# GLA norm ahead of the attention's splits, the window's pool lying first, and bonus rows loaded early, in a two-block fp32 kernel

## The chip, the cores and the metric

The kernel runs on one core of one Trainium2 chip. The metric is device time in microseconds; the time before is 2362.28 us, the median of three runs.

## The reference, cut to what matters

Two blocks run on a sequence of 1024 rows of width 1024, all in fp32. The first block (differential and stick-breaking attention, cross attention, MLP) is not touched by the change. The second block projects a normed input and mixes three things, whose outputs stand side by side in front of the last product:

```python
attn = _sliding_window_attention(aq, ak, av, sinks) * silu(ag)   # window of 128, bias by distance, a sink per head
rwkv = _rwkv7_mixer(h, rr, rk, rv, ...) * silu(rg)               # y + bonus, recurrence over time
gla = _gla_mixer(h, gq, gkk, gv, ...) * silu(gg)                 # gated linear attention, 4 heads
y = jnp.concatenate([attn, rwkv, gla], axis=-1) @ w_out
return x + gate[:, None] * _rmsnorm(y, g_post)
```

Linear attention (GLA) ends with a norm of its own: `o = o * rsqrt(mean(o*o, -1) + 1e-5) * norm_w`, with the mean over the 64 values of a head.

## The kernel before, in words

**Arithmetic.** Large products are made of three matmuls (`mm3`, L208 to L210) on operands split into a high part (ACT copies it, L200 for weights) and the rest (a subtraction, L201, on POOL in the second block). A weight piece comes by a DMA into `stg`, is split into `wh` (8 buffers, hence four pieces), and feeds twelve matmuls. PSUM has 8 banks.

**Order of work.** The second block runs its 1024 rows in two halves (c = 0, 1). The work is written as generators that issue instructions and yield costs; `weave(main, fill, ratio)` lets a filling stream of products (projections, output products) run beside a main stream that is a chain of small steps. The order of the main parts is: `g_rec(0)` (RWKV, then GLA, of the first half), the first attention window, `g_rec(1)`, and the second window with the output product (`g_tail`). At build time a scheduler orders each engine's instructions from this; on the chip each engine's queue runs in that order. All loads and stores are issued by SP, in one queue in order.

**A half of the recurrences.** `g_rec` opens the pool `rp` (with RWKV's tile `XT`), and when the first part is through, `gp` for GLA behind it. RWKV's `out(pr)` (L1910 on) loads two bonus rows (from `bd` and `pd`, tiles "t2"), multiplies them into the two output rows `yf` (L1917, L1918) and stores these to `yd`. GLA makes its score tile AT level by level, seven levels: `dist` (L2096 to L2098), `rows` (L2104), `gram` (L2115: 16 small matmuls a level, into one bank for each head, shared by two levels), `put` (L2127: a masked copy of each head's bank into AT). Then come a transpose (L2164, copied by L2166), the state (L2173 to L2179) and the output (L2186, L2189, copied out by L2193) into slots 4 and 5 of an eight-slot tile, `s.go`, whose slots 0 to 3 held AT.

**The norm.** `g_gla_out` (L2200 on) squares the output (L2209, ACT, into es), sums it by matmuls (L2214), takes the power (POOL, L218), broadcasts (L2217, ACT, into rb), multiplies by gate rows (sg, loaded by SP; L2220), makes rows of the broadcast by 8 matmuls on the identity (L2225), multiplies (L2226) and stores to `yd`. Its es, sg and rb are three tiles of tag "wp" from the window's pool `mx`.

**A window.** `win_load` loads one K row and four Q rows (`ws` tiles, also tag "wp"; in the second window also the last 128 columns of the half before) and splits them: `stack_k` (L455, L456 on ACT, L457 on DVE) and four `stack_q` (L441 twice on ACT, L442 twice on DVE). `g_window` issues the 1 MB bias table into slots 0 to 3 of `s.go`, runs the norm, and then eight units (`w_units`: 4 blocks of 128 rows by 2 groups of heads). A unit has scores (L1664, L1665), bias and maximum (L1667, L1668), exponentials (L1675), a normalisation of "wp" (L1681 on ACT for two heads, L1682 on POOL for two), transposes (L1696, copied by L1699), the product with V (L1706) and the gate (L1708).

**Where the window's pool lies.** In the first window `pp` (filling work: RWKV's preparation for the other half) is opened outside of `mx`, so `mx` lies behind it, over GLA's tiles. `g_window0` draws all of `win_load` in one go ahead of everything and yields -2000:

```python
with s.tc.tile_pool(name="mx", bufs=1, reuse_waits="tile") as mx:
    for _ in s.win_load(mx, 0):
        pass
    yield -2000
    yield from s.g_window(0)
```

In the second window `g_tail` allocates the tile `yw` first, runs `win_load` with its yields, then `g_window(1)`.

Of the kernel before, what the change touches and what calls it, by code (L numbers as in the profile page):

```python
# [12 lines left out]
F32 = mybir.dt.float32  # L13
F32R = mybir.dt.float32r
# [8 lines left out]
P = 128  # L23
D = 1024
T = 1024
KT = D // P
CH = 512
# [109 lines left out]
def chain(*gens):  # L137
    for g in gens:
        yield from g
# [29 lines left out]
class K:  # L169
# [1118 lines left out]
    def block2(s, wp, pre, out):  # L1288
        tc, nc = s.tc, s.nc
        with tc.tile_pool(name="b2", bufs=1, reuse_waits="tile") as b2, tc.tile_pool(name="wk3", bufs=2, reuse_waits="tile") as s.wk, tc.tile_pool(  # L1290
            name="smC", bufs=4, reuse_waits="tile"
        ) as s.sm:
            s.vt = b2.tile([P, NB, 400], F32, name="vt")
            s.b2_consts(b2)
            with tc.tile_pool(name="lo", bufs=1, reuse_waits="tile") as s.lop:
                with tc.tile_pool(name="wt", bufs=1, reuse_waits="tile") as wt:
                    with tc.tile_pool(name="pp", bufs=2, reuse_waits="tile") as pp:
                        vt = s.vt_load(wt, wp)

                        def beside(m):  # L1300
                            if m == 1:
                                hi = s.tl(s.xp, [P, KT, CH], "act", F32R)
                                lo = s.lop.tile([P, KT, CH], F32R, tag="lo1", name="lo1")
                                s.slow = s.fin_steps(1, hi, lo, s.wk)
                            for _ in range(2 if m >= 2 else 0):
                                next(vt, None)
                            if m == 7:
                                for _ in vt:
                                    pass

                        for _ in chain(s.g_p2a(pp, 0, pre, beside), s.g_vt()):
                            pass
                rest = s.g_p2b(1)
                weave(
                    s.g_rec(0), chain(s.g_p2b(0), s.take(rest, s.K0)),
                    0.25
                )
                with tc.tile_pool(name="pp", bufs=2, reuse_waits="tile") as pp:
                    weave(
                        s.g_window0(), chain(s.g_p2a(pp, 1), s.take(rest, s.K1)),  # L1320
                        0.9
                    )
                    while s.steps:
                        s.steps.pop(0)()
                tp = ExitStack()

                def tail():
                    yield from s.g_tail(tp.enter_context(tc.tile_pool(name="tp", bufs=1, reuse_waits="tile")))

                main = chain(s.g_rec(1), tail())  # L1330
                rest = chain(rest, s.g_wout2(b2), s.g_wout2a(s.g_final0(b2, out)))
                weave(main, rest, 0.28, False)
                with tp, tc.tile_pool(name="fp", bufs=1, reuse_waits="tile") as fp:
                    s.finish(fp, wp, out, rest)
# [253 lines left out]
    def win_load(s, mx, c):  # L1588

        nc = s.nc  # L1590
        sink = mx.tile([P, 8], F32, name="sink")
        s.nc.sync.dma_start(sink, s.A["sink"])
        kst = [mx.tile([P, P + CH], F32R, name=s.nm("k2")) for _ in range(4)]
        q8 = s.tl(s.xp, [P, KT, CH], "act", F32R)
        st = [mx.tile([P, 2, CH], F32, tag="wp", name=s.nm("ws"), bufs=3) for _ in range(3)]
        t = [st[i // 2][:, i % 2, :] for i in range(6)]
        if c == 1:
            s.nc.sync.dma_start(t[5][:, :P], s.pd[s.AK * P : (s.AK + 1) * P, c * CH - P : c * CH])
        s.get_rows(t[4], s.pd, s.AK, c)
        for h in range(4):  # L1600
            s.get_rows(t[h], s.pd, s.AQ + h, c)
        yield 0
        if c == 1:
            s.stack_k(mx, t[5][:, :P], [k[:, :P] for k in kst])
        s.stack_k(mx, t[4], [k[:, P:] for k in kst])
        yield 0
        qst = []
        for h in range(4):
            qst.append(s.stack_q(mx, t[h], [q8[:, 2 * h, :], q8[:, 2 * h + 1, :]]))
            yield 0  # L1610
        s.win = mx, sink, kst, qst

    def g_window(s, c):

        one = s.go
        bias = one[:, 0:4, :].rearrange("p a (h w) -> p (a h) w", w=2 * P)
        s.nc.sync.dma_start(bias, s.A["c_bias"])
        mx, sink, kst, qst = s.win
        yield from s.g_gla_out(mx, c)
        if c == 1:  # L1620
            t = s.lop.tile([P, KT, CH], F32R, tag="lo1", name=s.nm("ya"))
            s.ya = s.y_rows([4, 5, 6, 7], 1, [t, t])
        tail = []
        first = [(2500, 2150)[c], (3130, 2500)[c]] + [0] * 6
        yield from s.g_units(s.w_units(mx, c, qst, kst, bias, sink, one), tail, first)
        yield from s.g_drain(tail)

    def g_window0(s):
        with s.tc.tile_pool(name="mx", bufs=1, reuse_waits="tile") as mx:
            for _ in s.win_load(mx, 0):  # L1630
                pass
            yield -2000
            yield from s.g_window(0)

    def g_tail(s, tp):

        s.yw = tp.tile([P, KT, CH], F32R, name="yw")
        for x in s.win_load(tp, 1):
            yield x
        yield from s.g_window(1)  # L1640

    def w_units(s, wn, c, qst, kst, bias, sink, one):

# [82 lines left out]
    def g_rec(s, c):  # L1726

        tile = dict(bufs=1, reuse_waits="tile")
        with s.tc.tile_pool(name="rp", **tile) as rp:
            with s.tc.tile_pool(name="ra", **tile) as ra:  # L1730
                early, late = s.rwkv(rp, ra, c)
                yield from early
            with s.tc.tile_pool(name="gp", **tile) as gp:
                gla = s._gla(gp, c)
                for x in late:
                    yield x
                    for _ in range(2):
                        yield next(gla, 0)
                yield from gla

    def rwkv(s, rp, ra, c):
# [17 lines left out]
        st = {"S": rp.tile([P, 2, HD], F32, tag="S", name=s.nm("S"), bufs=2)}  # L1759
# [139 lines left out]
        def s5(jj):  # L1899
# [9 lines left out]
                )  # L1909
            del s2[jj]  # L1910

        def out(pr):
            y = st["yf"][pr]
            bo, sg = s.tl(s.wk, [P, CH], "t2"), s.tl(s.wk, [P, CH], "t2")
            s.get_rows(bo, s.bd, pr, c)
            s.get_rows(sg, s.pd, s.RG + pr, c)
            V.scalar_tensor_tensor(y, bo, 0.5, y, ALU.mult, ALU.add)  # L1917
            V.tensor_tensor(y, y, sg, ALU.mult)  # L1918
            s.put_rows(s.yd, 4 + pr, c, y)
# [99 lines left out]
                out(pr)  # L2019
                yield 0  # L2020

        return early(), late()


    def g_gate(s, c):
# [171 lines left out]
        yield -1500  # L2197
        s.go = one

    def g_gla_out(s, pool, c):  # L2200

        nc = s.nc
        V, G = nc.vector, nc.gpsimd
        mm, act = nc.tensor.matmul, nc.scalar.activation
        es, sg, rb = [pool.tile([P, 2, CH], F32, tag="wp", name=s.nm("go"), bufs=3) for _ in range(3)]
        es, sg, o = [[t[:, i, :] for i in range(2)] for t in (es, sg, s.go[:, 4:6, :])]
        rb = rb.rearrange("p a (b y t) -> p (a b) y t", y=2, t=P)
        for z in range(2):
            act(es[z], o[z], AF.Square)  # L2209
        yield -2500  # L2210
        ps = s.ps([P, 4, 2, 2])
        for z, e in enumerate(es):
            for i in range(4):
                mm(ps[:, i, z, :], e[:, i * P : (i + 1) * P], s.b64[:, 0:65:64], start=True, stop=True)  # L2214
        r = s.sm.tile([P, 16], F32, tag="gr", name=s.nm("gr"))
        s.rsq(r, ps.rearrange("p a b c -> p (a b c)"), 1.0 / HD, 1e-5)
        act(rb.rearrange("p i z (h t) -> p (i z h) t", t=HD), r[:, :, None].to_broadcast([P, 16, HD]), AF.Copy)  # L2217
        for z in range(2):
            s.get_rows(sg[z], s.pd, s.GG + z, c)
            V.scalar_tensor_tensor(o[z], o[z], s.hv[:, 8:9], sg[z], ALU.mult, ALU.mult)  # L2220
        yield -8000
        for z in range(2):
            ps = s.ps()
            for i in range(4):
                mm(ps[:, i * P : (i + 1) * P], rb[:, i, z, :], s.ident, start=True, stop=True)  # L2225
            V.tensor_tensor(o[z], o[z], ps, ALU.mult)  # L2226
            s.put_rows(s.yd, 6 + z, c, o[z])
            yield 872
# [184 lines left out]
```

## Time and profile before

| | us |
|---|---|
| runs of the kernel before (three) | 2349.17, 2362.28, 2364.81 |
| median | 2362.28 |
| the profiled execution | 2355.43 |
| its span, first to last instruction | 2353.7 |

The profiled execution's span is 1.7 us below its time; all starts below are microseconds from the start of the span. PE is TensorE's matmuls, ACT ScalarE, DVE VectorE, POOL GpSimd, SP the engine that issues the transfers. In a timeline row "x6" means six instructions in a row, the second number is the time from the first's start to the last's end, and a bracket tells the idle time of the engine just ahead and what ended it. The granted clock is that of TensorE, 1.00 being full.

### The profile page before, as it was taken

What the parts mean: (1) busy time and instruction counts of PE and PEld (TensorE: products, weight loads), DVE (VectorE), ACT (ScalarE), POOL (GpSimd) and SP (SyncE); (2) the same over time, 40 slices, a digit from 0 to 9 for tenths busy, and PEclk for the clock granted to TensorE, in tenths of its full rate; (3) what the DMA queues carried; (4) which work ended last, traced back from release to release, by engine and by line L of the source; (5) the groups of instructions that cost most, each with busy time, mean ns of one, the idle gap of its engine ahead of it and who ended that gap; (6) DMA issues with size and microseconds to landing.
All of it is one profiled execution on the core that took longest, in us unless ns stands there. A gap on an engine that the chain in (4) does not pass through costs nothing. (4 is left out here: it accounts for less than half of the span.)

```text
span 2353.7 us, 34778 instructions
## 1 busy us (share of the span) xinstructions
PE 2243.8 (95%) x13056; PEld 1897.6 (81%) x13056; DVE 1288.1 (55%) x2312; ACT 1034.8 (44%) x2196; POOL 688.9 (29%) x1035
## 2 busy tenths in 40 slices
PE   8999999999999999999999999999999988999876
PEld 6898999988898888888888888887787776777655
DVE  6665656676754555422423422346845648656485
ACT  6655656674643424411311312344533337434463
POOL 4101100000400003565655650036322333224343
PEclk9999999999999999999999999999999889989898
DMA  4010010123241311222222221143333233443461
GB/s 135 23 46 23 28 41 28 46 77 123 65 140 54 99 36 50 75 76 74 80 76 79 76 68 51 49 134 121 120 121 103 92 99 108 145 143 102 145 214 37
DMA packets 116393, 200.06 MB, mean 85 GB/s; under 512 B 14048, under 2 KB 33792, under 8 KB 115456
## 3 DMA queue, kind: packets, MB, share of 16 engines
q1 hardware_dynamic: 111456, 184.72, 24.0%
q0 software_dynamic: 4768, 13.11, 1.8%
q8 instruction: 102, 1.67, 0.3%
q14 instruction: 67, 0.55, 0.1%
HBM read 163.70 MB, written 34.08 MB: 84 GB/s over the span
## 5 line engine op out<-in xcount | busy, mean ns | idle before, releaser
L208 PE MATMUL ps<-act,wh 128*128 128x512 f32 x1664 | 668.3, 404 | 9.4 <-ACT wh L200 5.5
L210 PE MATMUL ps<-act,wh 128*128 128x512 f32 x1664 | 659.4, 396 | 0.0
L209 PE MATMUL ps<-act,wh 128*128 128x512 f32 x1480 | 584.0, 395 | 3.2 <-DVE act L204 2.1
L200 ACT ACTIVATE wh<-stg 128x512 fp32r<-128x512 f32 x374 | 234.4, 629 | 593.5 <-PE ps L209 472.6
L208 PEld LDWEIGHTS ps<-act,wh 128*128 128x128 f32 x1664 | 318.6, 192 | 80.5 <-ACT wh L200 5.5
L210 PEld LDWEIGHTS ps<-act,wh 128*128 128x128 f32 x1664 | 318.3, 191 | 68.9 <-issue 0.5
L209 PEld LDWEIGHTS ps<-act,wh 128*128 128x128 f32 x1480 | 282.2, 191 | 60.9 <-DVE act L204 3.0
L201 DVE TENSOR_TENSOR wh<-stg,wh 128x512 fp32r<-128x512 f32 x260 | 197.0, 760 | 154.9 <-ACT wh L200 152.1
L201 POOL TENSOR_TENSOR wh<-stg,wh 128x512 fp32r<-128x512 f32 x114 | 158.3, 1393 | 348.8 <-ACT wh L200 315.5
L907 DVE TENSOR_TENSOR act<-ps,act 128x512 f32<-128x512 f32 x112 | 77.0, 689 | 176.7 <-PE ps L210 176.5
L546 DVE TENSOR_TENSOR_SCAN pw<-pw,zero 128x128 f32<-128x128 f32 (+7 forms) x64 | 86.8, 1357 | 82.9 <-POOL pw L542 78.1
L944 POOL TENSOR_TENSOR ad<-ad,cb 128x256 f32<-128x256 f32 x96 | 72.8, 759 | 143.0 <-DMA ad<-adaT 139.9
L247 POOL TENSOR_TENSOR nacc<-nacc,t 128x512 f32<-128x512 f32 x28 | 38.5, 1378 | 259.9 <-ACT t L246 255.5
L1144 DVE SCALAR_TENSOR_TENSOR t<-ps,Rm 128x512 f32<-128x512 f32 x64 | 44.0, 691 | 128.3 <-PE ps L210 127.6
L949 POOL TENSOR_TENSOR ad<-ad 128x128 f32<-128x128 f32 (+5 forms) x288 | 98.9, 343 | 16.8
L208 PE MATMUL ps<-hid,wh 128*128 128x512 f32 x256 | 101.2, 395 | 0.0
L210 PE MATMUL ps<-hid,wh 128*128 128x512 f32 x256 | 101.2, 395 | 0.0
L209 PE MATMUL ps<-hid,wh 128*128 128x512 f32 x256 | 101.0, 395 | 0.0
L1145 ACT ACTIVATE t<-t 128x512 f32<-128x512 f32 x64 | 40.4, 631 | 135.8 <-DVE t L1144 135.8
L208 PE MATMUL ps<-wh,act 128*128 128x256 f32 x320 | 96.1, 300 | 0.0
L210 PE MATMUL ps<-wh,act 128*128 128x256 f32 x320 | 91.5, 286 | 0.0
L209 PE MATMUL ps<-wh,act 128*128 128x256 f32 x320 | 91.2, 285 | 0.0
(512 smaller groups left out, 4658.5 us busy)
## 6 DMA issues: line engine op xcount, KB each, us to landing
stg<-w2f SPq DMA_DIRECT2D x84, 256.0 KB, 3.0
stg<-w_dn SPq DMA_DIRECT2D x80, 256.0 KB, 2.8
stg<-w_up SPq DMA_DIRECT2D x64, 256.0 KB, 2.8
ad<-adaT POOLq DMA_DIRECT2D x96, 128.0 KB, 2.6
stg<-w2o SPq DMA_DIRECT2D x32, 256.0 KB, 2.8
pd<-t SPq DMA_DIRECT2D x30, 256.0 KB, 2.3
t<-yd SPq DMA_DIRECT2D x26, 256.0 KB, 3.4
rkd<-RK SPq DMA_DIRECT2D x4, 1280.0 KB, 5.2
```

Of the source, the lines that this page charges most:

```text
L200: nc.scalar.activation(hi, src, AF.Copy)
L201: (eng or nc.vector).tensor_tensor(lo, src, hi.bitcast(F32), ALU.subtract)
L208: mm(out, lh, rh, start=first, stop=False)
L209: mm(out, lh, rl, start=False, stop=False)
L210: mm(out, ll, rh, start=False, stop=last)
L247: nc.gpsimd.tensor_tensor(acc, acc, t[:, :n], ALU.add)
L546: V.tensor_tensor_scan(m[:, :w][:, ::-1], m[:, :w][:, ::-1], s.zero.to_broadcast([P, w]), 1.0, ALU.mult, ALU.add)
L907: s.nc.vector.tensor_tensor(hh, ps, hh, ALU.add)
L944: tt(t, t, cb[:, 256 * y : 256 * y + 256], ALU.mult)
L949: tt(acc[:, n, z, :] if w == 2 else a, a, b, ALU.add)
L1144: V.scalar_tensor_tensor(t, ps, 0.0, R[:, c * CH : (c + 1) * CH], ALU.max, ALU.mult)
L1145: nc.scalar.activation(t, t, AF.Square)
```

## The change

Three things are changed. `mx` is opened ahead of `pp`, and `win_load` allocates its load tiles ahead of everything else in it. `g_window` now drives `win_load` and `g_gla_out` by turns: loads; squares; K splits; norm sums, power, broadcast and gate; Q splits; then the rest of the norm and, behind it, the bias table's load. `g_gla_out` takes its es, rb and sg from slots 0 and 1, 2 and 3, 6 and 7 of `s.go`. The bonus rows of RWKV's first output row are loaded into tiles of their own ("ro") as soon as `gp` is open; those of the second row are loaded in `out(1)` as before.

```diff
-                with tc.tile_pool(name="pp", bufs=2, reuse_waits="tile") as pp:
+                with tc.tile_pool(name="mx", bufs=1, reuse_waits="tile") as mx, tc.tile_pool(
+                    name="pp", bufs=2, reuse_waits="tile"
+                ) as pp:
                     weave(
-                        s.g_window0(), chain(s.g_p2a(pp, 1), s.take(rest, s.K1)),
+                        s.g_window(0, mx), chain(s.g_p2a(pp, 1), s.take(rest, s.K1)),
...
     def win_load(s, mx, c):
...
+        st = [mx.tile([P, 2, CH], F32, tag="wp", name=s.nm("ws"), bufs=3) for _ in range(3)]
+        t = [st[i // 2][:, i % 2, :] for i in range(6)]
         sink = mx.tile([P, 8], F32, name="sink")
...
-    def g_window(s, c):
+    def g_window(s, c, mx, yw=None):
 
         one = s.go
+        load, out = s.win_load(mx, c), s.g_gla_out(c)
+        yield next(load)
+        if yw:
+            s.yw = mx.tile([P, KT, CH], F32R, name="yw")
+        yield next(out)
+        yield next(load)
+        yield next(out)
+        for x in load:
+            yield x
+        yield from out
         bias = one[:, 0:4, :].rearrange("p a (h w) -> p (a h) w", w=2 * P)
         s.nc.sync.dma_start(bias, s.A["c_bias"])
         mx, sink, kst, qst = s.win
-        yield from s.g_gla_out(mx, c)
...
-    def g_window0(s):
...
     def g_tail(s, tp):
 
-        s.yw = tp.tile([P, KT, CH], F32R, name="yw")
-        for x in s.win_load(tp, 1):
-            yield x
-        yield from s.g_window(1)
+        yield from s.g_window(1, tp, True)
...
+        def rows(pr, t):
+            bo, sg = st["rows", pr] = t
+            s.get_rows(bo, s.bd, pr, c)
+            s.get_rows(sg, s.pd, s.RG + pr, c)
+
         def out(pr):
             y = st["yf"][pr]
-            bo, sg = s.tl(s.wk, [P, CH], "t2"), s.tl(s.wk, [P, CH], "t2")
-            s.get_rows(bo, s.bd, pr, c)
-            s.get_rows(sg, s.pd, s.RG + pr, c)
+            if pr == 1:
+                rows(1, [s.tl(s.wk, [P, CH], "t2") for _ in range(2)])
+            bo, sg = st["rows", pr]
...
-        es, sg, rb = [pool.tile([P, 2, CH], F32, tag="wp", name=s.nm("go"), bufs=3) for _ in range(3)]
+        es, rb, sg = [s.go[:, z : z + 2, :] for z in (0, 2, 6)]
```

The new lines shift the numbers: in the rows of the changed kernel the units' lines are 1 or 2 higher (L1696 is L1697), those of GLA 7 higher (L2127 is L2134, L2209 is L2216).

The first place is VectorE's queue at the end of the first GLA. Before, with the masked puts of levels 4 to 6 (their shapes end in 4x16, 2x32 and 64):

```order
L2127 COPY_PREDICATED act_16187<-gm_17200,ps_17666 128x4x4x16
L2127 COPY_PREDICATED act_16187<-gm_17200,ps_17667 128x4x4x16
L2127 COPY_PREDICATED act_16187<-gm_17200,ps_17664 128x4x2x32
L2127 COPY_PREDICATED act_16187<-gm_17200,ps_17665 128x4x2x32
L2127 COPY_PREDICATED act_16187<-gm_17200,ps_17666 128x4x2x32
L2127 COPY_PREDICATED act_16187<-gm_17200,ps_17667 128x4x2x32
L2127 COPY_PREDICATED act_16187<-gm_17200,ps_17717 128x4x64
```

And the same place of the changed kernel, where k and act on the left are the low parts of the window's K and Q rows:

```order
L2134 COPY_PREDICATED act_16187<-gm_17204,ps_17666 128x4x4x16
L457 TENSOR_TENSOR k_3185_17822<-ws_17817,k_3183_17820 64x512
L2134 COPY_PREDICATED act_16187<-gm_17204,ps_17667 128x4x4x16
L457 TENSOR_TENSOR k_3186_17823<-ws_17817,k_3184_17821 64x512
L442 TENSOR_TENSOR act_17824<-ws_17815,act_17824 64x512 x4
L442 TENSOR_TENSOR act_17824<-ws_17816,act_17824 64x512 x4
L2134 COPY_PREDICATED act_16187<-gm_17204,ps_17664 128x4x2x32
L2134 COPY_PREDICATED act_16187<-gm_17204,ps_17665 128x4x2x32
```

Ten subtractions of the window's splits, which stood behind the whole of GLA, now stand ahead of the puts of its last two levels.

The second place is ScalarE's queue around the squares of the first window's norm. Before:

```order
L2193 ACTIVATE act_16187<-ps_17792 128x512
L455 ACTIVATE k_3180_17817<-ws_17824 64x512
L456 ACTIVATE k_3180_17817<-ws_17824 64x512
L455 ACTIVATE k_3181_17818<-ws_17824 64x512
L456 ACTIVATE k_3181_17818<-ws_17824 64x512
L200 ACTIVATE wh_17933<-stg_17931 128x512
L1448 ACTIVATE t_3201_17918<-ps_17869 64x512
L441 ACTIVATE act_17821<-ws_17822 64x512 x4
L441 ACTIVATE act_17821<-ws_17823 64x512 x2
L2209 ACTIVATE go_17883<-act_16187 128x512 x2
L441 ACTIVATE act_17821<-ws_17823 64x512 x2
```

In the changed kernel (L2173 is the copy of GLA's transpose, L2200 the copy of its output, L2216 the squares):

```order
L441 ACTIVATE act_17824<-ws_17815 64x512 x4
L441 ACTIVATE act_17824<-ws_17816 64x512 x4
L200 ACTIVATE wh_17836<-stg_17833 128x512
L2173 ACTIVATE act_16187<-ps_17750 128x512
L200 ACTIVATE wh_17843<-stg_17840 128x512
L200 ACTIVATE wh_17907<-stg_17905 128x512
L2200 ACTIVATE act_16187<-ps_17778 128x512
L2216 ACTIVATE act_16187<-act_16187 128x512
L2200 ACTIVATE act_16187<-ps_17792 128x512
L2216 ACTIVATE act_16187<-act_16187 128x512
```

The splits moved ahead of GLA's transpose, and each half of the squares stands right behind its copy.

The third place is ScalarE's queue at the end of the first window, where pt is RWKV's preparation for the other half and wp a unit's probabilities. Before:

```order
L1529 ACTIVATE pt_18759<-pt_18566 128x512
L1527 ACTIVATE pt_18525<-pt_18566 128x512
L1528 ACTIVATE pt_18631<-pt_18631 128x512
L1673 ACTIVATE wt_18569<-wt_18569 128x4
L1675 ACTIVATE wp_18568,wt_18569<-wp_18568,wt_18569 128x256 x4
L1523 ACT_TABLE_LOAD
L1523 ACTIVATE pt_18539<-pt_18539 128x512
L200 ACTIVATE wh_18707<-stg_18705 128x512
L1582 ACT_TABLE_LOAD
L1582 ACTIVATE t_3347_18695<-ps_18613 128x512
L1681 ACTIVATE wp_18477<-wp_18477,wt_18478 128x256 x2
L1681 ACTIVATE wp_18568<-wp_18568,wt_18569 128x256 x2
```

In the changed kernel:

```order
L1682 ACTIVATE wp_18463<-wp_18463,wt_18464 128x256 x2
L200 ACTIVATE wh_18698<-stg_18696 128x512
L1531 ACTIVATE pt_18755<-pt_18592 128x512
L1529 ACTIVATE pt_18527<-pt_18592 128x512
L1530 ACTIVATE pt_18632<-pt_18632 128x512
L1674 ACTIVATE wt_18551<-wt_18551 128x4
L1676 ACTIVATE wp_18550,wt_18551<-wp_18550,wt_18551 128x256 x4
L1525 ACT_TABLE_LOAD
L1525 ACTIVATE pt_18584<-pt_18584 128x512
L1700 ACTIVATE act_16187<-ps_18636 128x512
L1700 ACTIVATE act_16187<-ps_18642 128x512
L1682 ACTIVATE wp_18550<-wp_18550,wt_18551 128x256 x2
```

The normalisation of the first of these two units moved from behind the exponentials and both table loads to ahead of them; that of the next stands behind one load.

## Rows read from the trace of the kernel before

**Rows 1.** Page, part 1: busy us (share of the span), instructions.

```profile
PE 2243.8 (95%) x13056; PEld 1897.6 (81%) x13056; DVE 1288.1 (55%) x2312; ACT 1034.8 (44%) x2196; POOL 688.9 (29%) x1035
```

**Rows 2.** Waits of PE, 1850 to 2354: us in total, times, longest.

```profile
PE ps L1696 <- ACT wp L1681: 10.6, 2, 8.5
PE ps L2115 <- ACT t L246: 7.7, 1, 7.7
PE ps L2214 <- ACT go L2209: 6.6, 1, 6.6
```

**Rows 3.** Timeline of PE: start, us, operation, count, idle before and releaser.

```profile
1887.79 4.66 PE L2115 MATMUL ps<-gX 32*128 32x64 f32 x64
...
1917.76 1.86 PE L2214 MATMUL ps<-b,go 128*128 128x2 f32 x8 [6.64 <-ACT go L2209]
1919.48 0.77 PE L208 MATMUL ps<-act,wh 128*128 128x512 f32 x1
...
1923.45 0.40 PE L208 MATMUL ps<-act,wh 128*128 128x512 f32 x1
...
1924.15 0.95 PE L2214 MATMUL ps<-b,go 128*128 128x2 f32 x8
```

**Rows 4.** Stretches: us; PE, PEld, DVE, ACT, POOL busy (count); clock; DMA share, GB/s.

```profile
1883.60:1896.00 12.40, 12.40 (x85) 10.33 (x85) 5.71 (x17) 1.86 (x3) 1.26 (x1) 0.50 0.13 44
1917.80:1923.00 5.20, 5.20 (x16) 4.47 (x17) 2.63 (x4) 2.20 (x4) 0.00 (x0) 0.50 0.02 3
2003.00:2008.50 5.50, 5.50 (x19) 4.73 (x19) 4.03 (x8) 1.55 (x4) 0.00 (x0) 0.50 0.32 95
2193.00:2203.00 10.00, 10.00 (x36) 8.10 (x37) 8.05 (x15) 4.80 (x8) 1.97 (x2) 0.50 0.14 51
```

**Rows 5.** Timeline of ACT, splits and squares of the first window.

```profile
1913.16 3.89 ACT L441 ACTIVATE act<-ws 64x512 fp32r<-64x512 f32 x6
1917.08 1.15 ACT L2209 ACTIVATE go<-act 128x512 f32<-128x512 f32 x2
```

**Rows 6.** Timeline of SP, stores of RWKV and loads of the window.

```profile
1880.95 2.71 SPq L1387 DMA_DIRECT2D yd<-yf  x2
...
1906.37 3.41 SPq L1390 DMA_DIRECT2D ws<-pd  x5
```

**Rows 7.** DMA of L1390, 1906 to 1910: the five rows of the window.

```profile
DMA to landing us min/median/max: 2.9/4.0/4.4
```

**Rows 8.** Timeline of DVE, second product and first use of the bias.

```profile
1935.86 0.68 DVE L2226 TENSOR_TENSOR act<-act,ps 128x512 f32<-128x512 f32 x1
...
1940.04 0.40 DVE L1667 SCALAR_TENSOR_TENSOR wp<-ps,act 128x256 f32<-128x256 f32 x1
```

**Rows 9.** Timeline of DVE, four masked puts.

```profile
1889.90 1.48 DVE L2127 COPY_PREDICATED act<-gm,ps 128x256 f32<-128x256 int32 x4 [3.43 <-PE ps L2115]
```

**Rows 10.** Timeline of ACT, table load and logarithm of the first window's end.

```profile
1998.00 1.28 ACT L1523 ACT_TABLE_LOAD   x1
1999.29 0.63 ACT L1523 ACTIVATE pt<-pt 128x512 f32<-128x512 f32 x1
```

**Rows 11.** Timeline of ACT, second transition.

```profile
2185.95 0.31 ACT L455 ACTIVATE k<-ws 64x128 fp32r<-64x128 f32 x1 [5.62 <-DMA ws<-pd]
...
2192.18 0.59 ACT L246 ACTIVATE t<-ps 128x512 f32<-128x512 f32 x1
```

**Rows 12.** Timeline of SP, second transition.

```profile
2182.28 0.43 SPq L1598 DMA_DIRECT2D ws<-pd  x1
```

**Rows 13.** Timeline of DVE, second transition.

```profile
2174.84 1.07 DVE L1917 SCALAR_TENSOR_TENSOR yf<-t,yf 128x512 f32<-128x512 f32 x1 [5.00 <-DMA t<-bd]
```

**Rows 14.** DMA of L1617, the bias table, both windows.

```profile
DMA to landing us min/median/max: 4.8/4.8/4.8
```

**Rows 15.** Timeline of DVE, second window: second product, first use of the bias.

```profile
2228.49 0.69 DVE L2226 TENSOR_TENSOR act<-act,ps 128x512 f32<-128x512 f32 x1 [0.20 <-PE ps L2225]
...
2231.75 1.29 DVE L1667 SCALAR_TENSOR_TENSOR wp<-ps,act 128x512 f32<-128x512 f32 x2 [1.13 <-PE ps L1665]
```

More of the change, by code (lines that the diff above doesn't have):

```diff
@@ L1594, in win_load @@
         q8 = s.tl(s.xp, [P, KT, CH], "act", F32R)
-        st = [mx.tile([P, 2, CH], F32, tag="wp", name=s.nm("ws"), bufs=3) for _ in range(3)]
-        t = [st[i // 2][:, i % 2, :] for i in range(6)]
         if c == 1:
@@ L1626, in g_window @@
         yield from s.g_drain(tail)
-    def g_window0(s):
[L1629 to L1633, printed above, removed]
     def g_tail(s, tp):
-        s.yw = tp.tile([P, KT, CH], F32R, name="yw")
-        for x in s.win_load(tp, 1):
-            yield x
-        yield from s.g_window(1)
+        yield from s.g_window(1, tp, True)
     def w_units(s, wn, c, qst, kst, bias, sink, one):
@@ L1730, in g_rec @@
             with s.tc.tile_pool(name="ra", **tile) as ra:
-                early, late = s.rwkv(rp, ra, c)
+                early, late, rows = s.rwkv(rp, ra, c)
                 yield from early
@@ L1734, in g_rec @@
                 gla = s._gla(gp, c)
+                rows(gp)
                 for x in late:
@@ L2020, in late @@
                 yield 0
-        return early(), late()
+        return early(), late(), lambda gp: rows(0, [gp.tile([P, CH], F32, name=s.nm("ro")) for _ in range(2)])
     def g_gate(s, c):
@@ L2198, in _gla, with g_gla_out @@
         s.go = one
-    def g_gla_out(s, pool, c):
+    def g_gla_out(s, c):
         nc = s.nc
```

## The prediction

> **What bounds the kernel now.** I read the page first. TensorE (PE) is busy for 2243.8 us, 95% of the span [rows 1], so the whole kernel has about 110 us in which PE does nothing, and a change that neither adds nor removes matmuls can only move those and the clock. Next the waits of PE from 1850 us on, where nearly all the changed code runs [rows 2]: the three largest single ones are 8.5 us for the normalised probabilities (wp, L1681), 7.7 us for a square sum of the filling matmuls (t, L246) and 6.6 us for the squares of the GLA norm (go, L2209). Then the timelines of PE and of the engine named, to see what stood ahead of the instruction waited for. In [rows 3] the reader is to see that PE starts again at 1917.76 after 6.64 us and then runs at half speed: from 1919.48 to 1923.45 its nine matmuls start 0.44 us apart, at a granted clock of 0.50 [rows 4], the lower of the two levels (1.2 of 2.4 GHz). Eight of the norm's small matmuls take 1.86 us there and 0.95 a little later. So a long wait costs more than its length: with half of the 3.97 us and of the 1.86, this spell lost 2.8 us. The wait at the end of the first window is followed by 5.5 us at 0.50 too [rows 4]; half of that is again about 2.8.
>
> **The norm ahead of the splits, first window.** Why does PE stand until 1917.76? ScalarE (ACT) runs the k splits, then six q splits in one row (3.89 us from 1913.16), and only then the two squares [rows 5]. The squares need nothing but the GLA output, which ACT copies out of PSUM ahead of the k splits. The splits come so late because SP issues the loads of k and q at 1906.37 [rows 6]: their tiles lie over the GLA's own and wait for its end. After the change the pool lies over the RWKV tile, free long before, so SP can issue them right behind the two stores of the RWKV output. Those ended at 1883.66 [rows 6]; both halves are now multiplied in a row, so I take the loads to go out at about 1882.6. They land 2.9 to 4.4 us after [rows 7], the first at 1885.5. The squares then stand directly behind the copies that they read. Gain: 6.6 us of wait and 2.8 us of half clock, 9.4.
>
> This has a price. The twelve splits on ACT (0.65 us apart [rows 5]) now run from 1885.5 to about 1893.3, and the last of their ten subtractions on VectorE (DVE; 0.69 us, as another operation of 512 columns takes [rows 8]) ends at about 1894. In DVE's queue they now stand ahead of the last eight masked puts of the GLA. The first four of those ran from 1889.90, 1.48 us together [rows 9]. The last grams of the fourth head write a PSUM bank that the first of these puts must have read. PE ran its 64 grams from 1887.79 to 1892.45 [rows 3] and comes to these at some 1891.9; it can go on only at 1894.4. Price: 2.5 us of waiting, with PE at 0.50 there already [rows 4]. The clock was back at about 1896 [rows 4], and I take it to come back later by as much, 2.7 us more of half speed. The four bonus operations now run in a row ahead of the puts that end the short wait just before: 0.6 us. Sum of the price 5.8. Bounds: 0, if the rows land early enough for VectorE to be through by 1890, and 12.5, worked out under the rivals. Net for this place: 3.6 us gained, between 9.4 gained and 3.1 lost.
>
> A weight piece that ACT split in these 7.8 us now stands behind the splits. I cost this at nothing, because the eight weight buffers hold four pieces, of twelve matmuls each, and PE is on grams for 4.7 us meanwhile [rows 3]. Without that cover the cost is up to 5.8 us.
>
> **The end of the first window.** PE waits 8.5 us [rows 2] for a normalisation that ACT runs only behind three exponentials of the RWKV preparation, the exponentials of the next unit, a table load at 1998.00, a logarithm, a weight piece, a second table load and a copy. All of that ran back to back; the order of ACT's queue makes the wait, not its work. In the new order this unit's normalisation comes before that block, and the next unit's stands behind one table load, the logarithm and two copies, with 21 filling matmuls for PE meanwhile (4.9 us, at the 0.23 us a step that the three from 1923.45 to 1924.15 show [rows 3]). I take 1.5 us as left of the wait, and no half clock: 8.5 + 2.8 - 1.5 = 9.8 gained. Bounds: all 11.3 go, or the wait turns up again at the next unit (nothing gained). The load itself takes 1.28 us, and the logarithm starts 0.01 us behind its end [rows 10]. The Trainium skill (ScalarE: Activation LUTs, section What ACT_TABLE_LOAD costs) gives 1283 ns for a load and adds a drain of about 1380 ns to every switch. This trace agrees with the first number and shows no gap for the second. By the page's 2.66 us the wait left would be 1.4 us longer, and this term 8.4.
>
> **The second transition.** Here the splits stood ahead of the norm as well, but PE had filling work beside them and no wait at the norm. What PE waits for is the square sum of a filling product, 7.7 us [rows 2], which ACT runs at 2192.18, behind all k splits and two q splits [rows 11]. ACT could begin only when the rows landed, 5.62 us idle until 2185.95 [rows 11], and SP issued their loads from 2182.28 [rows 12], late because VectorE stood 5.0 us for the first bonus row, until 2174.84 [rows 13]. Now the first pair is in place early. The other pair takes its place in SP's queue, so VectorE still starts at 2174.84, but has both halves done by about 2177.3, with the puts behind them 0.65 us earlier; stores and loads follow, the loads at about 2177.9, 4.4 us earlier. ACT gains these 4.4 us and loses 3.9, because six more q splits now stand ahead of the square sum. So this wait changes by 0.5 us. With the 0.65 on the puts I take 1.2 gained; bounds 4.4 gained and 3.9 lost.
>
> **The bias table.** It lies where the squares and broadcast rows are now, so SP issues its 1 MB only behind the broadcast matmuls. In the first window that is just before VectorE's second product at 1935.86; it lands 4.8 us after issue [rows 14], and the first use was at 1940.04 [rows 8]: 1 us late, of which VectorE, with other preparation to do, passes on half. In the second window the second product was at 2228.49 and the first use at 2231.75 [rows 15]; with the stores ahead of it the table lands at about 2234.5, 2.8 us late. Behind the waiting operation on VectorE stand the splits of the output rows that the filling work needs next. I take 1.0 of the 2.8, nearer to nothing, because the fill in hand lasts for some matmuls more. Together 1.5 lost; bounds 0 and 3.8. The early bonus rows add no bytes. The end of the second window is reordered in small ways; I leave its waits as they are, within 3 us either way.
>
> **Sum.** 3.6 + 9.8 + 1.2 - 1.5 = 13.1 us. Against the profiled execution: 2355.43 - 13.1 = 2342.3. The timed runs' median is 6.9 us above it, which would give 2349.2. The four executions spread over 15.6 us, so I put the forecast between the two, at 2346. About 1%, 23.6 us, is what a measurement of this kernel can tell from no change; the forecast lies inside.
>
> **Rivals.** (a) The wait only moves. Nothing is left of the 9.8 at the end of the window, because the next unit's normalisation meets the table loads in place of this one's. For it speaks that both loads are still there, against it the order. Then 3.6 + 1.2 - 1.5 = 3.3 are gained: 2355 between the same two bases.
> (b) Slower: the splits in VectorE's queue, at the last puts of the GLA in both transitions. If the rows land 4 us later than I take them (their queue holds two stores and a weight piece ahead), VectorE is through at 1898, PE waits 6.5 us and has some 6 us more of half clock, 12.5 where 9.4 are gained. The second place pays the 3.9 us of the six splits and 2.5 of clock behind it, with no norm wait to gain. With (a) this is 9.4 - 12.5 - 6.4 - 1.5 = 11 us slower: 2370. It turns to a loss where the puts are held for more than some 4 us at each place.
> (c) The clock. If half of the low stretches at both transitions goes as well (12.4 and 10.0 us at 0.50 [rows 4], 11 us in all) and the price of the splits (5.8) does not appear, 13.1 + 11 + 5.8 = 30 are gained: 2329. For it speaks that the norm's wait leaves no trace in the clock once it is short, against it that the short waits before the low stretches stay.
> (d) The change does not do what it says: the loads stay behind the GLA because of another tile. The order puts the splits ahead of the puts, so this could only be a late landing, and is in (b).
>
> **How the numbers follow.** Forecast 0.55, own range 2336 to 2356; (a) 0.22; (b) 0.10; (c) 0.13. The range takes in (a), part of (b) above and part of (c) below: 2332 to 2365. Slower by over 1% (above 2386) needs more than (b): 0.03. Faster by over 1% (below 2338.7) is (c) and the lower edge of the forecast: 0.17. Within: 0.80.
>
> **What would show it.** Right: no wait at the norm sums (now L2221), the k splits on ACT before 1890, a new wait of 2 to 4 us at the last grams (now L2122) released by a masked put, no wait over 3 us at the transposes (now L1697) near 2000, the wait for t at L246 still 6 to 8 us long. Wrong: a gram wait over 6 us in the first window, a wait of 8 us for wp at the next unit, VectorE standing for the bias table for over 3 us.

## The result, and the profile after

Nine timed runs of the changed kernel have a median of 2372.76 us, nine of the kernel before beside them 2354.55: a ratio of 1.0076, 95% interval 1.0059 to 1.0093, some 18 us slower. The forecast was 2346, 13 us of gain, and the measured time lies above its range. The 2362.28 at the start was the median of three of these nine; by all nine the profiled execution of the kernel before (2355.43) lies at the median, not 6.9 us below it. In microseconds below, a ratio is multiplied with 2355.

First the page, part 1, of the changed kernel; its span is 2368.9 us, and the row answers to [rows 1]:

```profile
PE 2253.9 (95%) x13056; PEld 1907.2 (81%) x13056; DVE 1289.0 (54%) x2312; ACT 1033.8 (44%) x2196; POOL 688.3 (29%) x1035
```

The matmuls are the same 13056; PE is busy 10 us longer (a lower clock) and idle 5 us longer (2368.9 - 2253.9 = 115.0, before 109.9). Then the waits of PE from 1850 us on (in total, times, longest), which answer to [rows 2]:

```profile
PE ps L1707 <- ACT act L1700: 12.2, 8, 6.1
PE ps L1697 <- ACT wp L1682: 11.8, 3, 5.7
PE ps L2122 <- DVE act L2134: 9.3, 4, 4.7
PE ps L2122 <- ACT t L246: 5.7, 1, 5.7
PE ps L1777 <- DMA rk<-rkd: 4.2, 1, 4.2
PE ps L1979 <- ACT act L1973: 3.6, 1, 3.6
...
PE ps L1825 <- ACT act L1980: 2.1, 1, 2.1
```

The wait for the squares (6.6 us before) is not among them. New are a gram wait of 4.7 (third row), a wait for a DMA (rk), two in RWKV's inverse (L1979 and L1825) and, in the second row, one for wp at the first unit of the first window, where before none was over 1.5 us. The timeline of PE shows where they lie:

```profile
1890.09 1.96 PE L2122 MATMUL ps<-gX 32*128 32x64 f32 x14 [4.66 <-DVE act L2134]
...
1911.06 0.39 PE L210 MATMUL ps<-act,wh 128*128 128x512 f32 x1
1911.29 0.95 PE L2221 MATMUL ps<-b,act 128*128 128x2 f32 x8
...
1947.32 0.48 PE L1697 MATMUL ps<-ident,wp 128*128 128x128 f32 x1 [4.83 <-ACT wp L1682]
...
2006.02 3.78 PE L1707 MATMUL ps<-act,vt 128*128 128x512 f32 x4 [6.07 <-ACT act L1700]
...
2027.66 0.44 PE L1777 MATMUL ps<-ident,rk 128*128 128x128 f32 x1 [4.19 <-DMA rk<-rkd]
...
2095.68 3.62 PE L1979 MATMUL ps<-act 32*32 32x32 f32 x64 [3.57 <-ACT act L1973]
...
2102.50 2.82 PE L1825 MATMUL ps<-AV,act 64*64 64x128 f32 x12 [2.06 <-ACT act L1980]
```

At 1911.29 the norm's sums follow a filling matmul without a bracket, 0.23 us after it: that part did what it says. What ACT did before 2095.68 leads to a loss that the prediction has no term for. Timeline of ACT:

```profile
2092.34 0.63 ACT L200 ACTIVATE act<-t 128x512 fp32r<-128x512 f32 x1 [12.80 <-DMA t<-yd]
...
2095.03 1.07 ACT L1973 ACTIVATE act<-ps 32x512 f32<-32x512 f32 x2
```

ACT stood 12.80 us for a row of y, with the inverse's copy (L1973) queued behind it. Timeline of SP, which issues that load:

```profile
2076.35 0.33 SPq L280 DMA_DIRECT2D stg<-w2f  x1
2086.74 0.32 SPq L1392 DMA_DIRECT2D act<-pd  x1
2087.16 0.38 SPq L280 DMA_DIRECT2D stg<-w2f  x1
2087.59 0.90 SPq L1392 DMA_DIRECT2D t<-yd  x2
```

and VectorE's:

```profile
2082.89 3.83 DVE L1966 STREAM_TRANSPOSE act<-act 32x1024 f32<-32x1024 f32 x2
```

SP issues nothing from 2076.68 to 2086.74. The transfer at the head of its queue is `act<-pd`, the norm's second gate row for the second window, which lies in slot 7 of the shared tile since the change. That slot holds the inverse until the transposes at 2082.89 end, at 2086.72. Behind it stand the y rows, behind these ACT's copies, behind these PE. The Trainium skill (PSUM — Partial Sum Buffer, section Engine vs sequencer instructions) calls ScalarE's queue strict FIFO; the row at 2092.34 agrees, with 12.80 us.

Stretches of 15 us (columns as in [rows 4]), the two that hold these waits:

```profile
2091.00:2106.00 15.00, 9.38 (x88) 8.05 (x87) 3.42 (x4) 8.17 (x15) 5.47 (x4) 0.64 0.50 159
2106.00:2121.00 15.00, 14.75 (x125) 12.77 (x124) 3.66 (x11) 3.40 (x7) 0.00 (x0) 0.50 0.37 119
```

and the same work in the kernel before, where the inverse starts 0.55 us earlier:

```profile
2090.00:2105.00 15.00, 15.00 (x208) 12.73 (x207) 4.14 (x10) 5.92 (x11) 2.56 (x2) 0.98 0.49 150
2105.00:2120.00 15.00, 13.64 (x131) 11.71 (x125) 3.50 (x12) 4.67 (x11) 1.01 (x1) 0.66 0.01 5
```

PE did 88 instructions at a granted clock of 0.64 (between the two levels) where it had done 208 at 0.98, and the stretch behind ran at the lower level, 0.50.

### The profile page after: what moved, and what is told of

The parts are those of the page before. It is cut to its first block, busy times and chain, and to the rows that moved or that the text cites. A ratio compares the mean times of both kernels' runs of the same rounds, so it can differ in the third digit from the quotient of the medians.

```text
span 2368.9 us, 34765 instructions
## 1 busy us (share of the span) xinstructions
PE 2253.9 (95%) x13056; PEld 1907.2 (81%) x13056; DVE 1289.0 (54%) x2312; ACT 1033.8 (44%) x2196; POOL 688.3 (29%) x1035
## 4 chain that ended last, share of the span: by engine, by line
PE 81%; DVE 8%; ACT 4%; DMA 3%; issue 2%; POOL 1%; SPq 0%; DVEq 0%; POOLq 0%; ACTq 0%
PE ps L208 22%; PE ps L209 21%; PE ps L210 21%; PE ps L561 3%; PE ps L482 2%; DVE itmp L1952 1%; PE ps L468 1%; PE ps L469 1%; DVE act L1955 1%; PE ps L699 1%; PE ps L1707 1%; PE ps L1825 1%; DMA t<-yd 1%; ACT pw L675 1%; ACT wp L1676 0%
## 5 line engine op out<-in xcount | busy, mean ns | idle before, releaser
L1144 DVE SCALAR_TENSOR_TENSOR t<-ps,Rm 128x512 f32<-128x512 f32 x64 | 44.1, 691 | 127.4 <-PE ps L210 126.7
```

What stands on the lines that cost most here:

```text
L1144: V.scalar_tensor_tensor(t, ps, 0.0, R[:, c * CH : (c + 1) * CH], ALU.max, ALU.mult)
```

## The experiments

| run | what it is | ratio to before, 95% interval | us |
|---|---|---|---|
| changed kernel | | 1.0076 (1.0059 to 1.0093) | +17.9 |
| e1_gate_over_scores | changed, gate rows in other slots | 1.0033 (1.0016 to 1.0050) | +7.8 |
| e2_before_gate_in_slots | before, gate rows in slots 6, 7 | 1.0033 (1.0015 to 1.0050) | +7.8 |
| e3_no_early_bonus | changed, bonus rows late | 1.0088 (1.0065 to 1.0112) | +20.7 |
| e4_before_early_bonus | before, bonus rows early | 0.9995 (0.9974 to 1.0015) | -1.2 |
| f1_gate_and_old_pools | e1 with the old pool order | 0.9999 (0.9984 to 1.0014) | -0.2 |
| f2_second_window_as_before | e1 with the old second window | 1.0004 (0.9985 to 1.0023) | +0.9 |
| f4_pool_first_only | before, pool first | 1.0032 (1.0018 to 1.0046) | +7.5 |
| f5_both | f1 and f2 together | 0.9970 (0.9949 to 0.9990) | -7.1 |
| g1_both_no_early_bonus | f5, bonus rows late | 0.9982 (0.9963 to 1.0000) | -4.2 |
| g2_old_pools_only | changed, old pool order | 0.9981 (0.9966 to 0.9997) | -4.5 |

**The gate rows' slots.** The changed kernel with the gate rows over the scores and the broadcast rows in slots 6 and 7:

```diff
-        es, rb, sg = [s.go[:, z : z + 2, :] for z in (0, 2, 6)]
+        es, sg, rb = [s.go[:, z : z + 2, :] for z in (0, 2, 6)]
```

> The changed kernel with two slots exchanged: the gate rows sg lie over the scores (slots 2 and 3), the broadcast rows rb in 6 and 7. Theory S (SP's queue): in the changed kernel the load of the second gate row of the second half waits for the RWKV inverse that used slot 7 before it, at 2086.74, with SP idle for 10 us ahead of weight and output-row loads; here it waits for the end of GLA instead. S expects the 10 us gap in SP gone, no idle of over 4 us of PE between 2060 and 2110, the stretch from the first rk transpose to GLA's first gram back from 145 to 124 to 130 us, and 2352 to 2360 us in all (14 to 18 faster than the changed kernel). Rival W (the order of the first window and of the fill beside it leaves the RWKV of the second half without cover): the stretch stays at 140 to 146 us, the time within 3 us of 2372.

Measured: +7.8 us, 10 under the changed kernel, where theory S expected 14 to 18. Timeline of SP in e1:

```profile
2079.45 2.31 SPq L280 DMA_DIRECT2D stg<-w2f  x2
2083.50 0.80 SPq L1392 DMA_DIRECT2D t<-yd  x2
```

The gap is gone, and so are the waits at L1979 and for L1980. The stretch that theory S named, from the first rk transpose to the second half's first gram, takes 132.6 us, not the 124 to 130 expected. It took 145.5 in the changed kernel and 144.8 in e3, which also has the gate rows in slots 6 and 7, and 132.8 and 137.8 in f4 and f2 below, which have the pool first but not these slots.

The exchange does a second thing: the broadcast rows leave slots 2 and 3, where the bias table goes, so that the table is loaded earlier. VectorE's waits for the table in the changed kernel (0.87 and 5.71 us) are gone in e1, and so is PE's 4.83 us at the first unit. This rival has no run of its own. The stretches speak against it: from GLA's transpose to the first rk transpose PE takes 127.4 us in the changed kernel and 127.1 in e1, and the second window's units take 81.3 and 84.4. So 10 of the 18 us go with the exchange, and by these stretches with the gate row's load; the rest does not. The counterpart puts only the gate rows of the kernel before into the slots:

```diff
-        es, sg, rb = [pool.tile([P, 2, CH], F32, tag="wp", name=s.nm("go"), bufs=3) for _ in range(3)]
+        es, rb = [pool.tile([P, 2, CH], F32, tag="wp", name=s.nm("go"), bufs=3) for _ in range(2)]
+        sg = s.go[:, 6:8, :]
```

> The kernel before with its gate rows sg alone in slots 6 and 7 of the shared tile, all else as before. In its order the load of the second gate row stands some five loads later in SP's queue than in the changed kernel, behind two of the output-row loads. S expects a smaller dose: SP idle for 4 to 6 us until the inverse's transposes end (about 2086), 3 to 8 us slower than before in the stretch from the first rk transpose to GLA's first gram (126 us before). W expects no difference (within 2 us).

Measured: +7.8 us. Waits of SP in e2, 2060 to 2120 us:

```profile
SPq L1390 <- DVE act L1959: 6.5, 1, 6.5
```

SP stands 6.5 us for the inverse, a little over the 4 to 6 expected. Whether PE pays for it there isn't shown: from the first rk transpose to the second half's first gram it takes 134.81 us, which is 9 over the profile of the kernel before (125.73) and nothing over that of e4 (134.87), which has the old slots and no measurable loss. Beside e4 the loss comes later, mostly at the end: 85.45 us from the second window's first score to the last product with V, against 76.92. That stretch holds other "wp" tiles in another order now. As a proof of the gate's price this run is a miss.

**The bonus rows.** The changed kernel without the early load, then the kernel before with nothing but it (the lines of the change for `rows`):

```diff
-                rows(gp)
...
-            if pr == 1:
-                rows(1, [s.tl(s.wk, [P, CH], "t2") for _ in range(2)])
+            rows(pr, [s.tl(s.wk, [P, CH], "t2") for _ in range(2)])
```

> The changed kernel without its third part: both bonus rows are loaded in out() again. Theory S: nothing changes in the long stretch (still 140 to 148 us), the time is within 4 us of the changed kernel's 2372. If the early bonus rows are what disturbs SP's queue (rival R), the time falls by over 8 us.

```diff
-            bo, sg = s.tl(s.wk, [P, CH], "t2"), s.tl(s.wk, [P, CH], "t2")
-            s.get_rows(bo, s.bd, pr, c)
-            s.get_rows(sg, s.pd, s.RG + pr, c)
+            if pr == 1:
+                rows(1, [s.tl(s.wk, [P, CH], "t2") for _ in range(2)])
+            bo, sg = st["rows", pr]
```

> The kernel before with only the third part: first pair of bonus rows loaded early. By the prediction's reckoning it gains about 0.7 us on the puts and up to 4 at the second transition: 0 to 4 us faster than before. R expects over 4 us slower.

Measured: +20.7 and -1.2. The first lies 2.8 us above the changed kernel, with intervals that overlap; the second is no difference. The early rows are not the cause, and a gain from them isn't shown either.

**The pools' order.** e1 with the pools as before, and the kernel before with its window's pool first:

```diff
-                with tc.tile_pool(name="mx", bufs=1, reuse_waits="tile") as mx, tc.tile_pool(
-                    name="pp", bufs=2, reuse_waits="tile"
-                ) as pp:
+                with tc.tile_pool(name="pp", bufs=2, reuse_waits="tile") as pp, tc.tile_pool(
+                    name="mx", bufs=1, reuse_waits="tile"
+                ) as mx:
```

> The changed kernel with the gate rows' second load over the scores' slots (as in e1_gate_over_scores) and with the window's pool inside the projection's again, so that the splits stand behind GLA's puts on DVE and the first halves of the norm's squares ahead of them on ACT. Theory P (the splits ahead of the puts cost what the grams wait for, 4.66 us, and no more): the waits of the first grams go, from the first gram to the first transpose 35 to 38 us where e1 took 43.9, the wait of the norm's sums stays gone, and the time is 2357 to 2361, 4 to 8 under e1. Theory T (what is left of the loss is in the second window and its clock): 2362 to 2367, and the last stretch stays at 81 to 86 us.

```diff
-                with tc.tile_pool(name="pp", bufs=2, reuse_waits="tile") as pp:
+                with tc.tile_pool(name="mx", bufs=1, reuse_waits="tile") as mx, tc.tile_pool(
+                    name="pp", bufs=2, reuse_waits="tile"
+                ) as pp:
...
+        st = [mx.tile([P, 2, CH], F32, tag="wp", name=s.nm("ws"), bufs=3) for _ in range(3)]
+        t = [st[i // 2][:, i % 2, :] for i in range(6)]
         sink = mx.tile([P, 8], F32, name="sink")
```

> The kernel before with only the pool's place changed: the splits are no longer held back by the projection's pool and stand ahead of GLA's puts, the norm still follows all splits in tiles of the shared tag. Theory P: the grams wait 4 to 6 us as in the changed kernel, the norm's sums still wait (5 to 9 us), and the time is 2359 to 2364 beside 2355 to 2356 of before. Theory T or none: 2353 to 2358, what the grams lose is got back by the splits that are done earlier.

Measured: f1 8.0 us under e1, f4 7.5 over the kernel before: one price, found from both sides. In f1 the gram stretch takes 34.97 us (first gram to first transpose) where e1 took 43.90. Timeline of PE in f4:

```profile
1892.06 1.96 PE L2116 MATMUL ps<-gX 32*128 32x64 f32 x10 [6.19 <-DVE act L2128]
...
1912.42 0.72 PE L2215 MATMUL ps<-b,go 128*128 128x2 f32 x6
...
2026.49 0.30 PE L1776 MATMUL ps<-ident,rk 128*128 128x128 f32 x1 [3.85 <-DMA rk<-rkd]
```

The reader is to see three things. The grams wait for the masked put behind the splits, as in the changed kernel. The norm's sums do not wait (no bracket at 1912.42), against what was expected of f4: the splits are done so early that nothing of them is left ahead of the squares. And the DMA wait at rk belongs to the pool order as well; it stands in f4, e1, e3, f2 and the changed kernel (3.7 to 4.3 us) and is at most 0.7 in f1, f5, g1 and g2.

**The second window.** e1 with the second window's steps as before (all splits, then the norm in "wp" tiles, the bias loaded ahead):

```diff
+        if c == 1:
+            s.yw = mx.tile([P, KT, CH], F32R, name="yw")
+            for x in s.win_load(mx, c):
+                yield x
+            s.nc.sync.dma_start(bias, s.A["c_bias"])
+            yield from s.g_gla_out(c, mx)
...
+        if pool:
+            es, sg, rb = [pool.tile([P, 2, CH], F32, tag="wp", name=s.nm("go"), bufs=3) for _ in range(3)]
```

> e1_gate_over_scores with the second window in the order of before: all splits first, then the norm in tiles of the shared tag, its bias loaded ahead. Theory T (the new interleaving of the second window costs there): the stretch from the second window's first score to the last probability matmul falls from 84.4 to 76 to 79 us at a clock near 0.96, and the time is 2356 to 2360. Theory P (the loss that is left is the splits ahead of the puts in the first window): 2362 to 2367, and the last stretch stays above 81 us or what it gives is lost before it.

Measured: 6.9 us under e1. The last stretch, from the second window's first score to the last product with V, in e1:

```profile
2234.17:2318.56 84.39, 70.04 (x306) 52.03 (x305) 57.66 (x110) 49.76 (x136) 33.86 (x24) 0.86 0.49 162
```

and in f2:

```profile
2236.99:2313.59 76.60, 63.66 (x308) 47.05 (x307) 59.30 (x110) 49.82 (x136) 34.24 (x24) 0.96 0.55 177
```

Same work, 7.8 us less, 6.4 of them PE's busy time at a higher clock (0.96 for 0.86). With the new order (changed kernel, e1, e3, f1, g2) this stretch took 81.3 to 84.8 us in every profile, with the old one (before, e4, f2, f4, f5, g1) 76.6 to 80.8. The exception is e2, which has the old order and the gate rows in the slots, with 85.45. In e1 the clock falls three more times than in f2, each time behind a wait of PE: 3.24 us until 2273.24, 2.67 until 2297.66 and 4.28 until 2309.06. In f2 it stays at 1.00 from 2253 us to the end of the stretch, and no wait there is over 2.41.

f5 joins f1's pools, f2's second window and e1's slots. Of the change it keeps the first window's norm ahead of the splits and the early bonus rows:

> f1_gate_and_old_pools and f2_second_window_as_before together: the norm ahead of the splits in the first window alone, in parts of its own tile with the gate rows over the scores, the pools in their old order, the second window as before, the bonus rows early. Theories P and T both: neither the wait of the first grams nor the longer tail, 2345 to 2352, under the kernel before by what the norm's sums waited (6.6 us) less a little. If the freed wait comes back later as it did in the changed kernel (the score's copy 6.07 us near 2006): 2353 to 2358, the same as before.

Measured: -7.1 us, faster than both kernels, with no wait at the first window's last grams and none at the norm's sums. Timeline of PE in f5:

```profile
1906.37 0.95 PE L2231 MATMUL ps<-b,act 128*128 128x2 f32 x8
...
1999.65 3.78 PE L1715 MATMUL ps<-act,vt 128*128 128x512 f32 x4 [6.01 <-ACT act L1708]
```

At the window's end it still waits 6.01 us.

**One part undone, and one left out.** g1 is f5 with the same edit as in e3; g2 is the changed kernel with f1's edit alone, the gate rows staying in slots 6 and 7.

> f5_both without the early load of the bonus rows, so that the first window's norm ahead of the splits is alone against the kernel before. Theory N (what f5_both gains, some 7 us, is the norm's place alone; the bonus rows gave nothing in e4_before_early_bonus): 2347 to 2354. Theory B (in this order the early rows are worth the 5 us that e3_no_early_bonus lost): 2354 to 2359, no longer measurably under the kernel before, with the second transition's wait on the bonus's sum back.

> The changed kernel with only the pools' order undone: the splits stand behind GLA's puts, the gate rows stay in slots 6 and 7. In this order the second gate load stands only two loads of y and their weights ahead of its old place in SP's queue, not seven issues, as it did in the changed kernel. If the terms add up (splits ahead of the puts 8 us) and the gate's load costs by what stands behind it in SP's queue: 2358 to 2364, SP's idle time before the gate's load under 5 us where the changed kernel had 10, and no wait of the inverse's matmuls over 2 us there. If the gate's slot costs its 10 us wherever its load stands: 2366 to 2371.

Measured: -4.2 and -4.5 us. g1's distance from f5 is within the intervals, but its own interval reaches 1.0000, so this run decides neither for theory N nor for B. g2 is lower than either theory said: 22 us under the changed kernel by the pool order alone, more than any other edit gives back. With the pool in its old place nothing of the loss is left. Waits of SP in g2, 2045 to 2110 us:

```profile
SPq L1392 <- DVE act L1966: 6.8, 1, 6.8
```

In the changed kernel the same row says 10.0. SP still stands for the gate's slot (longer than the 5 us expected), but two loads of y are held behind it instead of four, and no matmul of the inverse waits over 1 us for ACT there. Whether the slot costs in this order isn't shown: f1 and g2 differ by 4.3 us, with intervals that overlap.

## Why the prediction was wrong

Two steps failed most: opening the pool first, which the prediction nets with the norm's gain as 3.6 us gained, and SP's queue, where one moved load has no term. A third term, the gain at the end of the first window, came in part at most.

**Norm ahead of the splits, 9.4 gained: right in the mechanism.** The wait of 6.64 [rows 3] is gone, and the matmuls behind it step 0.23 us apart again. f4 shows what the prediction missed: the pool lying first removes this wait by itself, and so does the norm's place without it (f1, g2). The change does both, and pays for the one it does not need.

**Splits ahead of the puts, 5.8 lost: the right place, sized too small.** The forecast wait of 2 to 4 us was 4.66, in e1 and f4 6.2, and the whole pool order costs 7.5 (f4) to 8.0 (e1 to f1), and 22 in the changed kernel (g2). In the sum of 5.8 the 2.7 us of half clock are counted whole, where the prediction elsewhere takes half of such a spell. The weight piece behind the splits, costed at nothing, brought no wait of PE; a DMA wait for rk of 4 us, some 130 us later, goes with this order and was not seen. Three stretches, from the first gram to the first rk transpose, show what the pool's place takes away. In the kernel before, in the changed kernel and in g2:

```profile
1854.70:2024.25 169.55, 147.33 (x836) 112.23 (x835) 105.66 (x227) 85.59 (x194) 54.51 (x46) 0.88 0.37 119
...
1849.00:2019.40 170.40, 149.87 (x844) 113.55 (x844) 110.91 (x231) 85.92 (x195) 53.90 (x46) 0.88 0.35 112
...
1855.40:2010.84 155.44, 143.37 (x837) 108.55 (x836) 109.00 (x228) 85.33 (x194) 55.64 (x46) 0.93 0.38 124
```

With the old norm and the old pools (before, e2, e4) it is 166.5 to 169.6 us, in the five kernels with the pool first 167.9 to 171.0, and with the new norm and the old pools (f1, f5, g1, g2) 155.4 to 163.1. Here the prediction counted 13.4 us of gain (3.6 and 9.8). The changed kernel shows none of it, and the same norm in the old pool order shows 3 to 14.

**End of the first window, 9.8 gained: wrong; the wait moved, as rival (a) said.** The wait of 8.5 [rows 2] became one of 6.07 at 2006.02, with ACT's copy behind the next unit's exponentials (not behind the table loads, as (a) had it), at a clock of 0.51 from 2003 to 2010. The price taken for it, "1.5 us as left of the wait, and no half clock", was the mis-sized term; f5 has 6.01 there too. Only in g2 it was small (2.2 and 1.7). At the first unit the table loads did make a wait that was not there before: the normalisation behind PE's 4.83 us at 1947.32 stands behind two of them.

**Second transition, 1.2 gained.** The wait for t went from 7.7 to 5.7 us, within its bounds.

**Bias table, 1.5 lost: near in the first window, not in the second.** Timeline of VectorE:

```profile
1931.28 0.76 DVE L1668 SCALAR_TENSOR_TENSOR wp<-ps,act 128x256 f32<-128x256 f32 x2 [0.87 <-DMA act<-c_bias]
...
2247.88 1.29 DVE L1668 SCALAR_TENSOR_TENSOR wp<-ps,act 128x512 f32<-128x512 f32 x2 [5.71 <-DMA act<-c_bias]
```

The first is near the 1 us worked out. In the second window VectorE stood 5.71 us, where 2.8 were worked out and over 3 was named as a sign of being wrong; PE then waited 2.45 us for a split of the output rows, the place that the prediction named. e3 and g2 have these waits too (7.1 and 7.5 us on VectorE in the second window); the runs of the changed kernel with the gate rows over the scores (e1, f1, f2, f5, g1) have none. Since g2 is no slower than f1, no run shows what they cost.

**SP's queue: left out.** The working follows the loads of k, q, the bonus rows and the bias table through SP's queue. The gate rows' load, which moves as well, is not in it, and so stands at nothing without a reason. It went into slots with another owner (slots 6 and 7 in the diff), its place in SP's queue went ahead of the y rows, SP stood 10.0 us for it, and 10 us of time (changed kernel to e1) go with it.

**End of the second window: "I leave its waits as they are, within 3 us either way".** It cost 6.9 us in both pairs (e1 to f2, f1 to f5), most of it by the clock in the last stretch. What in the new order makes the longer waits, behind which the clock falls there, is open; the changed kernel, e1, f1 and g2 each have one or two waits of 4.3 to 5.7 us for wp there, at one unit or another, where none for wp is over 2.3 in f2 and f5. g2, which keeps the new second window and is no slower than g1, shows that these terms don't simply add.

On the way from the changed kernel by e1, f1 and f5 to the kernel before, the steps are 10 (gate rows' slots), 8 (pool order), 7 (second window) and -7 (what f5 keeps), together 18. They add up because they are steps of one way, not because each part has that price: on the way by g2 the pool order alone is 22, and the slots give nothing back behind it. So the pool's place is the part that all of the loss needs, and the gate's 10 us are shown only where the pool lies first. Rival (b) named the right side and its place, for 11 us; the stall of SP was named by none of the rivals.

## What to carry to other kernels

When a tile is moved into slots that another step owns, look up every transfer that writes it: its place in the issuing queue, when the slot comes free, and what stands behind it. What a transfer costs that waits at the head of a queue hangs on when the loads behind it are due: with 10.0 us of SP standing and four loads of y behind it, ScalarE and then PE stood; with 6.8 us and two loads (g2) no matmul waited over 1 us for ScalarE there. Where two edits each remove the same wait, try each alone: one of them may bring only its price. And undo the parts one by one from the changed kernel too: here one of them alone gave back more than the whole loss.

## What the runs showed of the hardware that was not expected

Two profiled executions differ by 9 us over the same matmuls, with about the same idle time, by the granted clock. The stretch from the first rk transpose to the second half's first gram, in the kernel before:

```profile
2024.25:2149.98 125.73, 120.42 (x948) 97.00 (x946) 84.16 (x164) 53.64 (x103) 40.07 (x30) 0.93 0.37 119
```

and in e4, whose time isn't measurably different:

```profile
2018.91:2153.78 134.87, 128.94 (x947) 104.78 (x945) 85.33 (x164) 53.79 (x103) 39.45 (x30) 0.86 0.35 115
```

PE is idle for 5.3 and 5.9 us; the rest is its clock, 0.93 against 0.86 (948 and 947 instructions). Eight us of it, at the same distance from the start of the inverse, in the kernel before and in e4:

```profile
2097.37:2105.37 8.00, 7.95 (x120) 6.84 (x118) 3.37 (x10) 2.51 (x6) 0.32 (x1) 1.00 0.57 170
...
2093.00:2101.00 8.00, 8.00 (x58) 7.67 (x57) 1.94 (x5) 1.97 (x4) 0.24 (x1) 0.50 0.20 73
```

In e4 the clock fell to 0.50 at about 2092 us, though PE had been busy without a break from 2080 on, and came back at about 2123. Why it fell there is not shown. Of the other kernels with the old pool order, f1 took 126.8 us for the stretch, and e2, f5, g1 and g2 134.5 to 134.9. So one profile's stretch length is no price of an edit, unless its clock is read with it and timed runs agree.
